# Streamed attention in slots of a whole product half, with values, transposes and scores of two stages after it

## The chip, the cores and the metric

The kernel runs on one core of a Trainium2 chip. The metric is the device time of one execution in microseconds (us); a kernel's time is the median of several runs. TensorE (PE) does matmuls and transposes, VectorE (DVE) and ScalarE (ACT) element work, GpSimd (POOL) some of the splitting of weights, and SyncE (SP) issues most of the DMAs.

## The reference

One layer of a model with two branches, on 1024 tokens of width 1024, all in float32:

```python
h = rmsnorm(x, norm_g) * (1 + scale) + shift
glu_a, glu_b, z_conv, q, k, v, z_att, g_conv, g_att = split(h @ w_in)
u = causal_conv31(glu_a * sigmoid(glu_b)) + conv_b
y_conv = (silu(layernorm(u)) * silu(z_conv)) @ w_conv_out
q, k = partial_rope(q), partial_rope(k)          # 24 heads of 64, 16 of 64 columns turned
for (window, dilation) in ((128, 1), (512, 4), (2048, 16)):   # 8 heads each
    out, max, den = causal window attention on every dilation-th token
att = sum(den * exp(max - max_all) * out) / sum(den * exp(max - max_all))
y_att = (att * silu(z_att)) @ w_att_out
merged = sigmoid(g_conv) * y_conv + sigmoid(g_att) * y_att
out = rmsnorm(x + gate * (merged @ w_o), final_g)
```

## The kernel before

Every float32 matrix that is multiplied is split into a high and a low part, and a tile's product is made of three matmuls (hi·hi, lo·hi, hi·lo; mm3, L72 to L75). A half of a unit, 128 output rows by 512 tokens, is 8 such products of three, thus 24 matmuls, summed in one PSUM bank. "Product" below means one of these matmuls of 128x512.

The stages follow each other: the norm and v, the units of the convolution branch, its output projection, then the attention stage (from about 645 to 1138 us), the merge and the last projection. The change is in the attention stage. There PE has two kinds of work at once:

- **A stream of units** (`units`, `pieces`). First 12 pairs of key and query units, one for each n = (j, g), j = 0 to 3 being a pair of heads and g = 0 to 2 the group; part 0 holds the columns that rope turns, part 1 the others. Then 8 units of the gate. Each unit has two halves. A half's bank comes from the pool pd2, which has two banks; so a half's first product waits until the half before the last has been read. After a half, `Parts.__call__` reads the bank: for part 0 a shuffle (L709), two multiplications (L710 "rot", L711) and an addition (L712) on DVE; then for both parts the high part on ACT (L720) and the low one on DVE (L721) into the tile kqp. Here "sh" and "rot" come from two buffers of one tag. So the rot of a unit's second half must wait until L720 and L721 of its first half have read theirs. When both halves are made, SP moves them by DMA (L785) to the tiles that attention reads: k2 and q2, and q's low part to ql.
- **Attention** (`Attend`), for the units that are finished, in eight stages per n; each takes two tiles of 128 queries of one head. `scores` (L843, L844) makes a bank of scores; DVE adds the mask and takes the maximum (L847) and its negative multiple nm (L850); ACT takes exp (L852, one instruction per tile, 128 or 256 wide). `turn` transposes the result (L860), and DVE or ACT copies it to pt (L863, L865). `values` multiplies with v (L875). After g = 2, `combine` loads the three groups' results again and weighs them, in two halves: small DVE work on maxima and denominators (L897 to L913), three wide multiplications (L917) and two additions (L920, L922, result "pr"), then four transposes on PE (L926), a multiplication by the silu gate (L927) and a store to DRAM (L929).

Both are put together in a loop over slots. A slot before has 12 products (k = 0 to 3, or 4 to 7 of a half), then the scores of stage st, the transposes of stage st−2, the values of stage st−3, then steps of `combine` by the tables FIRST and SECOND, and at last the call that reads a bank if a half is complete. A unit is 13 slots ahead of its attention (LEAD). The order of PE is written out by hand (`manual_schedule`); the order of DVE, ACT, POOL and SP is set by the scheduler when the kernel is built, and each engine then runs its list strictly in that order, waiting on semaphores.

## Time and profile before

| what | us |
|---|---|
| median of 3 runs (1286.51 to 1288.05) | 1287.0 |
| the profiled execution | 1284.9 |
| its span | 1283.1 |
| PE busy | 1251.0 |
| DVE busy | 895.0 |
| ACT busy | 476.3 |
| PE busy in the stretch 700 to 1060 us (360.0 long) | 355.88 |

The times are of one execution that a profiler recorded. A row of a timeline gives the start, the duration, the engine, the line, and output<-inputs; what stands in brackets is the engine's idle time before the instruction and what ended it. Matmuls are pipelined: a product lasts 0.39 us in the record, and the next one starts 0.23 us after it. "PE s L844 <- DMA ql<-kqp" in the list of waits means that PE's matmul of line 844, which writes s, waited for that DMA.

### The profile page before, as it was taken

The numbers are of one execution on the slowest core, as the hardware profiler recorded it, in microseconds if no ns is written. First come the engines' busy times: TensorE is split into PE (matmuls) and PEld (weight loads), VectorE is DVE, ScalarE is ACT, GpSimd is POOL, SyncE is SP. The second block draws the span as 40 slices with busy tenths as digits, with TensorE's granted clock in tenths as the row PEclk, the third lists the DMA queues.
The fourth block names the chain that finished last, engine by engine and source line by source line (L and its number), as shares of the span: only waits on it lengthen the run. The fifth ranks groups of instructions, "written<-read, shape, count | busy, mean of one in ns | idle before, by whom it ended". The sixth has DMA issues, their size and how long they took to land.

```text
span 1283.1 us, 16610 instructions
## 1 busy us (share of the span) xinstructions
PE 1251.0 (97%) x6148; PEld 1050.6 (82%) x6148; DVE 895.0 (70%) x1568; ACT 476.3 (37%) x911; POOL 114.6 (9%) x86
## 2 busy tenths in 40 slices
PE   6999999999999999999999999999999989999997
PEld 4777888888888888888788888888888878887786
DVE  6777999999999986853245545766666654348544
ACT  4653112111222146620115545445545458333211
POOL 0000000000000000000132111111111002202200
PEclk9999999999999999999999999999999999999999
DMA  9522311211211122555675565576675565558322
GB/s 367 180 97 73 109 66 57 91 52 47 94 55 50 50 74 74 165 183 188 143 182 125 125 159 142 156 179 150 153 207 126 147 181 177 151 203 286 117 96 69
DMA packets 85525, 171.53 MB, mean 134 GB/s; under 512 B 11202, under 2 KB 41026, under 8 KB 85444
## 3 DMA queue, kind: packets, MB, share of 16 engines
q1 hardware_dynamic: 69024, 157.66, 42.1%
q10 hardware_dynamic: 16420, 12.80, 3.2%
q8 instruction: 49, 0.80, 0.3%
q14 instruction: 32, 0.26, 0.1%
HBM read 105.74 MB, written 33.23 MB: 108 GB/s over the span
## 4 chain that ended last, share of the span: by engine, by line
PE 86%; DVE 5%; DMA 3%; issue 2%; ACT 2%; SPq 1%; POOL 1%; POOLq 0%; ACTq 0%; DVEq 0%
PE d L73 20%; PE d L74 20%; PE d L75 20%; PE o L875 4%; PE d L466 2%; PE d L467 2%; PE d L465 2%; PE d L1060 2%; PE d L1061 2%; PE t L860 2%; PE d L1059 2%; PE s L844 1%; PE s L843 1%; PE d L249 1%; PE d L247 1%
## 5 line engine op out<-in xcount | busy, mean ns | idle before, releaser
L73 PE MATMUL d<-hh,whi 128*128 128x512 f32 x1072 | 428.0, 399 | 1.8 <-DVE rot L710 0.9
L74 PE MATMUL d<-hl,whi 128*128 128x512 f32 x1072 | 418.0, 390 | 1.8 <-DVE hl L347 1.8
L75 PE MATMUL d<-hh,wlo 128*128 128x512 f32 x1072 | 419.1, 391 | 0.0
L406 DVE SCALAR_TENSOR_TENSOR v<-u,cw,v 128x1024 f32<-128x1024 f32 x232 | 280.7, 1287 | 0.0
L75 PEld LDWEIGHTS d<-hh,wlo 128*128 128x128 f32 x1072 | 201.3, 188 | 43.7 <-POOL wlo L58 0.7
L74 PEld LDWEIGHTS d<-hl,whi 128*128 128x128 f32 x1072 | 201.9, 188 | 41.6 <-DVE hl L347 2.6
L73 PEld LDWEIGHTS d<-hh,whi 128*128 128x128 f32 x1072 | 201.8, 188 | 41.3 <-DVE rot L710 1.5
L57 ACT ACTIVATE whi<-wraw 128x512 fp32r<-128x512 f32 (+1 forms) x107 | 87.9, 834 | 272.6 <-PE d L74 236.0
L58 POOL TENSOR_TENSOR wlo<-wraw,whi 128x512 fp32r<-128x512 f32 (+1 forms) x56 | 84.5, 1525 | 659.1 <-ACT whi L57 557.2
L852 ACT ACTIVATE sb<-sb,nm 128x128 f32<-128x128 f32 (+1 forms) x192 | 85.0, 444 | 86.3 <-DVE nm L850 82.0
L847 DVE CUSTOM_DVE_ANT_0 sb<-s,mask 128x128 f32<-128x128 f32 (+1 forms) x192 | 59.8, 347 | 61.1 <-PE s L844 54.9
L875 PE MATMUL o<-vt,pt 128*128 128x64 f32 x560 | 73.5, 267 | 1.6 <-ACT pt L863 1.0
L875 PEld LDWEIGHTS o<-vt,pt 128*128 128x128 f32 x560 | 70.2, 192 | 2.6 <-ACT pt L863 1.3
L58 DVE TENSOR_TENSOR wlo<-wraw,whi 128x1024 fp32r<-128x1024 f32 (+1 forms) x51 | 60.2, 1183 | 15.1 <-ACT whi L57 14.6
L1060 PE MATMUL d<-ol,hh 128*128 128x512 f32 (+1 forms) x136 | 51.6, 380 | 3.0 <-POOL ol L58 3.0
L844 PE MATMUL s<-k,ql 128*128 128x128 f32 (+1 forms) x192 | 51.0, 279 | 2.9 <-DMA ql<-kqp 2.9
L1059 PE MATMUL d<-oh,hh 128*128 128x512 f32 (+1 forms) x136 | 51.4, 378 | 0.1
L1061 PE MATMUL d<-oh,hl 128*128 128x512 f32 (+1 forms) x136 | 51.4, 378 | 0.0
L467 PE MATMUL d<-vh,hl 128*128 128x512 f32 x128 | 49.8, 389 | 0.0
L73 PE MATMUL d<-uh,whi 128*128 128x512 f32 x128 | 49.8, 389 | 0.0
L466 PE MATMUL d<-vl,hh 128*128 128x512 f32 x128 | 49.8, 389 | 0.0
L74 PE MATMUL d<-ul,whi 128*128 128x512 f32 x128 | 49.8, 389 | 0.0
(213 smaller groups left out, 1738.6 us busy)
## 6 DMA issues: line engine op xcount, KB each, us to landing
wraw<-in_w_t SPq DMA_DIRECT2D x67, 512.0 KB, 4.1
k<-kqp SPq DMA_DIRECT2D x96, 128.0 KB, 2.6
q<-kqp SPq DMA_DIRECT2D x96, 128.0 KB, 2.4
wa<-in_w_ada SPq DMA_DIRECT2D x16, 512.0 KB, 5.9
rd<-oscr SPq DMA_DIRECT2D x8, 792.0 KB, 5.6
ql<-kqp SPq DMA_DIRECT2D x48, 128.0 KB, 2.4
wraw<-in_w_v SPq DMA_DIRECT2D x11, 512.0 KB, 3.6
x<-in_xT SPq DMA_DIRECT2D x8, 512.0 KB, 10.2
```

The lines of the kernel that those rows point to most:

```text
L57: nc.scalar.activation(hi, raw, AF.Copy)
L58: (lo_eng or nc.vector).tensor_sub(lo, raw, hi.bitcast(F32))
L73: nc.tensor.matmul(ps, lh, rh, start=start, stop=False)
L74: nc.tensor.matmul(ps, lh, rl, start=False, stop=False)
L75: nc.tensor.matmul(ps, ll, rh, start=False, stop=stop)
L406: nc.vector.scalar_tensor_tensor(d, u[:, k:k + S], cw[:, ct, k:k + 1], d, op0=mult, op1=add)
L466: nc.tensor.matmul(ps, hh[:, k, ts_], rl, start=False, stop=False)
L852: nc.scalar.activation(sb[:, c:c + w], sb[:, c:c + w], AF.Exp, bias=nm[:, t - tp:t - tp + 1], scale=SCALE, accum_out=ov[:, t, h, 64:65])
L875: nc.tensor.matmul(self.po[:, t % 4, h], pt[:, c + i:c + i + P], self.vt[:, kb, r], start=i == 0, stop=i + P == w)
L1059: nc.tensor.matmul(ps, hh[:, k, c], rh, start=k == 0, stop=False)
L1060: nc.tensor.matmul(ps, hh[:, k, c], rl, start=False, stop=False)
L1061: nc.tensor.matmul(ps, hl[:, k, c], rh, start=False, stop=k == KT - 1)
```

## The change

- A slot is a whole half, 24 products. After it come the values of two stages, then the transposes of two stages, then the scores of two stages; the transposes are one slot behind the scores and the values two.
- LEAD is 7 slots of 24, and the tables FIRST and SECOND are given in new slots; the steps of one combination that were in slots of their own now often share one.
- The moves of q's low part come as soon as part 1 of its unit is made; v is loaded apart, in the third slot of the attention before (`load_v`).
- In `combine` the store to atscr is a step of its own, a slot later; for j = 3 that step isn't run.

```diff
@@ -768,8 +768,6 @@
                 for k in range(KT):
                     c = slice(k * P, (k + 1) * P)
                     mm3(ps, hi[:, c], lo[:, c], hh[:, k, s], hl[:, k, s], k == 0, k == KT - 1)
-                    if k == 3:
-                        yield
                 yield lambda half=half, s=s, ps=ps: consume(half, s, ps)
 
     LOW, UP = slice(0, 64), slice(64, 128)
@@ -798,6 +796,8 @@
 
         for part in range(2):
             move(q_low[n % 2], 0, n, part, 1, 1)
+
+    def load_v(n):
         v2[n] = stk.tile([P, 8, P], F32, name="vt", tag="vt", bufs=2)
         v_load(v2[n], order[n][1], order[n][0])
         if order[n][1] == 0:
@@ -925,10 +925,10 @@
         for t in range(4):
             nc.tensor.transpose(pt[:, t * P:(t + 1) * P], pr[:, t].rearrange("p h c -> p (h c)"), ident)
         nc.vector.tensor_mul(at, pt, at)
-        if j < 3:
-            nc.sync.dma_start(atscr[j][:, s], at)
-        else:
+        if j == 3:
             att_parts(3, s, at)
+        yield
+        nc.sync.dma_start(atscr[j][:, s], at)
         yield
 
     ah, al = {}, {}
@@ -942,54 +942,53 @@
     stream = pieces()
 
 
-    LEAD, TURN, VAL = 13, 2, 3
-    stages = 8 * len(order)
-
-    FIRST, SECOND = (2, 6, 6, 7, 7, 9), (8, 11, 11, 12, 12, 14)
+    LEAD = 7
+    slots = 4 * len(order)
+
+    FIRST, SECOND = (1, 3, 3, 3, 4, 4, 5), (5, 6, 6, 6, 7, 7, 8)
     beside, heads = {}, {}
 
     with tc.manual_schedule(engines={nc.tensor.engine}):
-        for slot_ in range(-LEAD, (2 * len(order) + KT) * 4 - LEAD):
+        for slot_ in range(-LEAD, (2 * len(order) + KT) * 2 - LEAD):
             due, made[:] = made[:], []
             after = next(stream)
             for x in due:
                 move_kq(*x)
-                if x == (0, 1):
-                    load_low(0)
-            if 0 <= slot_ < stages:
-                n, st_ = divmod(slot_, 8)
-                if st_ == 0:
-                    heads[n] = Attend(n)
-                if st_ == 4 and n + 1 < len(order):
-                    load_low(n + 1)
-                heads[n].scores(st_)
-            if TURN <= slot_ < stages + TURN:
-                n, st_ = divmod(slot_ - TURN, 8)
-                heads[n].turn(st_)
-            if VAL <= slot_ < stages + VAL:
-                n, st_ = divmod(slot_ - VAL, 8)
-                heads[n].values(st_)
-                if st_ == 7:
-                    del heads[n]
-                    j, g = order[n]
-                    if g == 2:
-                        for half, steps in enumerate((FIRST, SECOND)):
-                            c = combine(j, half)
-                            for x in steps:
-                                beside.setdefault(slot_ + x, []).append(c)
+                if x[1]:
+                    load_low(x[0])
+                    if x[0] == 0:
+                        load_v(0)
+            n, pair = divmod(slot_, 4)
+            if 0 <= slot_ < slots and pair == 0:
+                heads[n] = Attend(n)
+            if 0 <= slot_ < slots and pair == 2 and n + 1 < len(order):
+                load_v(n + 1)
+            for back, what in ((2, Attend.values), (1, Attend.turn), (0, Attend.scores)):
+                if 0 <= slot_ - back < slots:
+                    n, pair = divmod(slot_ - back, 4)
+                    for st_ in (2 * pair, 2 * pair + 1):
+                        what(heads[n], st_)
+                    if back == 2 and pair == 3:
+                        del heads[n]
+                        j, g = order[n]
+                        if g == 2:
+                            for half, steps in enumerate((FIRST, SECOND)):
+                                c = combine(j, half)
+                                for x in steps[:6 if j == 3 else 7]:
+                                    beside.setdefault(slot_ + x, []).append(c)
             for c in beside.pop(slot_, ()):
                 next(c)
             for c in late:
-                for x in (2, 2, 3):
+                for x in (1, 1, 2):
                     beside.setdefault(slot_ + x, []).append(c)
             late[:] = []
-            j = slot_ - stages - VAL
+            j = slot_ - slots - 2
             if 0 <= j < 3:
                 raw = load_raw(atscr[j])
                 for half in range(2):
                     s = slice(half * 512, half * 512 + 512)
                     att_parts(j, s, raw[:, s])
-            if j == 11:
+            if j == 5:
                 ahead = weights(a["w_ao"][0], 512)
             if after:
                 after()
```

The slots X that the prediction speaks of are numbered so that the attention starts with slot 0; slot 4m+2 holds the second half of a part 0. The next rows are of slot 19, X+1 for X = 18, and the first product of slot 20. The numbers behind the names tell tiles apart and are other ones in the two kernels.

PE before, at the end of the half ahead of the product that takes up the bank: s are scores, t transposes (t_6346 of exps, t_6355 of a combination), o the values, d the bank of products:

```order
L843 MATMUL s_6334<-k2_5884,q2_5885 128x128
L844 MATMUL s_6334<-k2_5884,ql_4284 128x128
L860 MATMUL t_6346<-ident_66,sb_6234 128x128 x3
L875 MATMUL o_6317<-vt_5747,pt_6315 128x64 x3
L926 MATMUL t_6355<-ident_66,pr_6259 128x128 x4
L73 MATMUL d_6364<-hh_64,whi_6058 128x512
```

PE after, at the same place:

```order
L860 MATMUL t_6267<-ident_66,sb_6184 128x128 x3
L860 MATMUL t_6273<-ident_66,sb_6196 128x128 x3
L843 MATMUL s_6279<-k2_5531,q2_5532 128x128
L844 MATMUL s_6279<-k2_5531,ql_4283 128x128
L843 MATMUL s_6279<-k2_5531,q2_5532 128x256
L844 MATMUL s_6279<-k2_5531,ql_4283 128x256
L843 MATMUL s_6291<-k2_5531,q2_5532 128x128
L844 MATMUL s_6291<-k2_5531,ql_4283 128x128
L843 MATMUL s_6291<-k2_5531,q2_5532 128x256
L844 MATMUL s_6291<-k2_5531,ql_4283 128x256
L73 MATMUL d_6327<-hh_64,whi_6024 128x512
```

Scores were first and are now last, directly ahead of the product d_6327, whose bank is that of d_6136, the second half of the unit's part 0.

DVE before at this place; rot_6160 is of the unit's first half, rot_6262 of the second, and d_6167 the bank that d_6364 above takes up:

```order
L847 ISA sb_6300,ov_5930<-s_6299,mask_4268 128x256
L847 ISA ov_5930 128x1
L850 TENSOR_SCALAR nm_6301<-ov_5930 128x2
L721 TENSOR_TENSOR kqp_5870<-rot_6160,kqp_5870 128x512
L710 TENSOR_TENSOR rot_6262<-d_6167,ctab_3672 128x512
L712 TENSOR_TENSOR rot_6262<-rot_6262,sh_6261 128x512
L847 ISA sb_6335,ov_6333<-s_6334,mask2_4269 128x128
```

DVE after; the same two are rot_6129 and rot_6211, and d_6136 is the bank that d_6327 takes up:

```order
L850 TENSOR_SCALAR nm_6281<-ov_5952 128x2
L847 ISA sb_6292,ov_5952<-s_6291,mask_4268 128x256
L847 ISA ov_5952 128x1
L850 TENSOR_SCALAR nm_6293<-ov_5952 128x2
L721 TENSOR_TENSOR kqp_5842<-rot_6129,kqp_5842 128x512
L710 TENSOR_TENSOR rot_6211<-d_6136,ctab_3672 128x512
L712 TENSOR_TENSOR rot_6211<-rot_6211,sh_6210 128x512
L721 TENSOR_TENSOR kqp_5842<-rot_6211,kqp_5842 128x512
L721 TENSOR_TENSOR kqp_6034<-d_6225,kqp_6034 128x512
```

The reading of the bank (L710) stands behind L721 of the first half in both; ahead of it are now the reductions of the scores s_6279 and s_6291, which PE issues just ahead of the product that needs the bank.

ACT before at this place, with the high part of the first half (L720 of rot_6160):

```order
L852 ACTIVATE sb_6300,ov_5930<-sb_6300,nm_6301 128x128
L852 ACTIVATE sb_6300,ov_5930<-sb_6300,nm_6301 128x256
L720 ACTIVATE kqp_5870<-rot_6160 128x512
L720 ACTIVATE kqp_5870<-rot_6262 128x512
L720 ACTIVATE kqp_6068<-d_6276 128x512
```

ACT after:

```order
L852 ACTIVATE sb_6280,ov_5952<-sb_6280,nm_6281 128x128
L852 ACTIVATE sb_6280,ov_5952<-sb_6280,nm_6281 128x256
L852 ACTIVATE sb_6292,ov_5952<-sb_6292,nm_6293 128x128
L852 ACTIVATE sb_6292,ov_5952<-sb_6292,nm_6293 128x256
L720 ACTIVATE kqp_5842<-rot_6129 128x512
L720 ACTIVATE kqp_5842<-rot_6211 128x512
L720 ACTIVATE kqp_6034<-d_6225 128x512
```

The first half's L720, on which L721 above waits, has four exps of the slot's own scores ahead of it in place of two.

The third place is the second half of the first combination (j = 0). DVE before, where pr_6259 is the operand of the transposes t_6355 above:

```order
L865 COPY pt_6249<-t_6245 128x384
L850 TENSOR_SCALAR nm_6235<-ov_5930 128x2
L922 TENSOR_TENSOR pr_6259<-rd_6054 128x512
L711 TENSOR_TENSOR sh_6261<-sh_6261,stab_3673 128x512
L847 ISA sb_6300,ov_5930<-s_6299,mask_4268 128x128
```

DVE after, where pr_6398 is that operand, in slot 20:

```order
L917 TENSOR_TENSOR rd_6208<-rd_6208,w_6306 128x4x2x64
L850 TENSOR_SCALAR nm_6386<-ov_6352 128x2
L920 TENSOR_TENSOR rd_6208<-rd_6208 128x4x2x64
L922 TENSOR_TENSOR pr_6398<-rd_6208 128x512
L927 TENSOR_TENSOR at_6312<-t_6400,at_6312 128x512
L709 STREAM_SHUFFLE sh_6502<-d_6419 128x512
```

PE after, at the end of slot 20:

```order
L843 MATMUL s_6384<-k2_5868,q2_5869 128x128
L844 MATMUL s_6384<-k2_5868,ql_4284 128x128
L926 MATMUL t_6400<-ident_66,pr_6398 128x128 x4
L73 MATMUL d_6419<-hh_64,whi_6218 128x512
L74 MATMUL d_6419<-hl_65,whi_6218 128x512
```

The scores s_6384, their reductions on DVE, pr and the transposes of pr are in one slot now; before, the transposes were in a later slot than pr, and behind transposes and values.

## Prediction

> **What bounds the kernel now.** I read the page first: the busy table, then the chain that ended last.

> ```profile
> span 1283.1 us, 16610 instructions
> PE 1251.0 (97%) x6148; PEld 1050.6 (82%) x6148; DVE 895.0 (70%) x1568; ACT 476.3 (37%) x911; POOL 114.6 (9%) x86
> PE 86%; DVE 5%; DMA 3%; issue 2%; ACT 2%; SPq 1%; POOL 1%; POOLq 0%; ACTq 0%; DVEq 0%
> ```

> TensorE is busy for 97% of the span and carries 86% of the last chain. The change leaves each matmul in the program, so it can win only PE's idle time or the joints between matmuls, and lose by making PE wait. Next I read PE's waits in the stretch of attention (672 to 1066 us):

> ```profile
> PE s L844 <- DMA ql<-kqp: 2.9, 1, 2.9
> PE o L875 <- ACT pt L863: 1.0, 1, 1.0
> PE d L73 <- DVE rot L710: 0.9, 4, 0.3
> PE o L875 <- DVE pt L865: 0.5, 1, 0.5
> ```

> In 394 us PE waits 5.3 us. That is all that a better order can win there. The third row matters most: four products waited, 0.3 us at most, for the rope's first multiplication (L710), which reads the PSUM bank that the product wants. There are two such banks.

> Then the timeline of PE through one slot of before (start, duration, line):

> ```profile
> 700.24 0.39 PE L75 MATMUL d<-hh,wlo 128*128 128x512 f32 x1
> ...
> 700.82 0.28 PE L844 MATMUL s<-k,ql 128*128 128x256 f32 x1
> 700.94 0.60 PE L860 MATMUL t<-ident,sb 128*128 128x128 f32 x4
> 701.37 1.00 PE L875 MATMUL o<-vt,pt 128*128 128x64 f32 x8
> 702.19 0.48 PE L73 MATMUL d<-hh,whi 128*128 128x512 f32 x1
> 702.50 0.39 PE L74 MATMUL d<-hl,whi 128*128 128x512 f32 x1
> 702.73 0.39 PE L75 MATMUL d<-hh,wlo 128*128 128x512 f32 x1
> ```

> From the last score (700.82) to the next product (702.19) lie 1.37 us of transposes and values. This is the time that DVE and ACT get after a stage's scores before PE needs a product's bank; after the products of a half's first slot they get another slot of 12 products.

> **The change part by part.** *Joints.* The first product after values passes on after 0.31 us (702.19 to 702.50), the second after 0.23 (to 702.73). A slot of 24 has one such joint where two of 12 had two: 48 joints less at 0.08 us are −4 us (bounds −8, if the score side saves as much, and 0).

> *Waits of before.* q's low part is moved with its unit, so the row of 2.9 us should go, and two stages of distance cover the two pt rows, 1.5 us. The rot waits (0.9) are counted anew below. I take −5, bounds −6 and −2.

> *The bank of a rope's second half.* This is the main term. A half's products go to the bank that the half two slots earlier used. Where that was the second half of a part 0 (X = 2, 6, ... 38: ten places), the bank comes free with L710, which writes "rot" into a buffer that L721 of the first half must have read; L721 waits for L720 on ACT. The order of the engines, given above, has these behind slot X+1's reductions, and in part behind its exps. In before 12 products, transposes and values stood between; this is the chain at one such place:

> ```profile
> 772.23 0.28 PE L844 MATMUL s<-k,ql 128*128 128x128 f32 x1
> ...
> 773.20 0.17 DVE L850 TENSOR_SCALAR nm<-ov 128x2 f32<-128x2 f32 x1
> ...
> 773.40 0.40 ACT L852 ACTIVATE sb<-sb,nm 128x128 f32<-128x128 f32 x1 [0.23 <-DVE nm L850]
> ...
> 773.80 0.39 ACT L852 ACTIVATE sb<-sb,nm 128x128 f32<-128x128 f32 x1
> ...
> 774.19 1.11 ACT L720 ACTIVATE kqp<-rot 128x512 fp32r<-128x512 f32 x1
> ...
> 775.33 1.09 DVE L721 TENSOR_TENSOR kqp<-rot,kqp 128x512 fp32r<-128x512 f32 x1 [1.96 <-ACT kqp L720]
> ```

> ```profile
> 776.45 0.69 DVE L710 TENSOR_TENSOR rot<-d,ctab 128x512 f32<-128x512 f32 x1
> 777.20 0.50 PE L73 MATMUL d<-hh,whi 128*128 128x512 f32 x1 [0.19 <-DVE rot L710]
> ```

> From the last score to the product it needed 772.23 to 777.20, 4.97 us, of which PE waited 0.19, since it had 4.8 us of other work. In after this work has gone to the other side: values and transposes come first, then two stages of scores, then at once the product. So the chain is a wait nearly as long as itself: about 4.97 less 0.2 that a product follows a score by anyway, 4.8.

> It varies with the unit and the order. Units of group 0 (X = 6, 18, 30) are contiguous and cheaper, and 256-wide tiles dearer:

> ```profile
> 844.86 0.63 ACT L720 ACTIVATE kqp<-rot 128x512 fp32r<-128x512 f32 x1 [1.13 <-DMA ql<-kqp]
> 845.52 0.69 DVE L721 TENSOR_TENSOR kqp<-rot,kqp 128x512 fp32r<-128x512 f32 x1 [2.81 <-ACT kqp L720]
> 846.25 0.69 DVE L710 TENSOR_TENSOR rot<-d,ctab 128x512 f32<-128x512 f32 x1
> 846.81 0.61 PE L926 MATMUL t<-ident,pr 128*128 128x128 f32 x4
> ```

> ```profile
> L847 DVE CUSTOM_DVE_ANT_0 sb<-s,mask 128x256 f32<-128x256 f32 x88 | 35.2, 420 | 21.1 <-PE s L844 21.1
> L847 DVE CUSTOM_DVE_ANT_0 sb<-s,mask 128x128 f32<-128x128 f32 x94 | 24.8, 285 | 31.7 <-PE s L844 25.5 <-PE t L860 6.1
> ```

> Contiguous saves 1.11−0.63 and 1.09−0.69, 0.9 us. The two stages of a slot queue on DVE: their eight short instructions add some 0.3 us of backlog at 285 ns tiles, and three 256-wide ones another 0.14 each. By the position of the first half's L720 on ACT:
> - behind all four exps (X = 10, 18, 26, 30): 5.0, 4.6, 5.8, 4.6, which is 4.8 plus backlog 0.2 to 1.0, less 0.9 and plus 0.7 for the contiguous ones with wide tiles: 20.0;
> - behind the first exp only (X = 2, 38): an exp less, 4.3 each: 8.6;
> - ahead of the exps (X = 14, 22): only the reductions (1.0), L721 (1.1) and L710 (0.7) with a little backlog are left, 3.1 each: 6.2;
> - a slot earlier, so that only L710 stands behind the reductions (X = 6, 34): 1.2 and 1.8: 3.0.

> Sum +38. Bounds: 33 if there is no backlog of the two stages, 44 if each place has a full backlog of a stage's reductions (0.6 us).

> *The combination's second half.* In after the four transposes L926 stand right behind the slot's scores (slots 20, 32, 44), and DVE computes their operand pr (L922) behind the same scores' reductions. In before:

> ```profile
> 833.61 0.28 DVE L847 CUSTOM_DVE_ANT_0 sb<-s,mask 128x128 f32<-128x128 f32 x1
> ...
> 834.89 0.32 DVE L913 TENSOR_TENSOR w<-w,wd 128x8 f32<-128x8 f32 x3
> 835.12 1.89 DVE L917 TENSOR_TENSOR rd<-rd,w 128x512 f32<-128x512 f32 x3
> 837.05 0.69 DVE L920 TENSOR_TENSOR rd<-rd 128x512 f32<-128x512 f32 x1
> ...
> 838.84 0.55 DVE L865 COPY pt<-t 128x384 f32<-128x384 f32 x1
> ...
> 840.19 0.68 DVE L922 TENSOR_TENSOR pr<-rd 128x512 f32<-128x512 f32 x1
> ```

> pr was ready at 840.87, its transposes ran at 846.81: 6 us of cover, so it cost nothing. In after DVE has from the end of the slot's transposes to do: the copy 0.55, then a stage's reductions with w, wd and L917 (833.61 to 837.01, 3.4), the second stage's reductions 0.75, L920 0.69, L922 0.68: 6.1 us. Scores of two stages are eight matmuls 0.12 us apart (700.82 to 700.94), 1.0 us, and a hop is 0.2: PE waits 6.1−1.0−0.2 = 4.9, in slots 20 and 32. In slot 44 the whole chain from ma on stands behind both stages' reductions: 1.3 us after the last score, then 3.9 for w, wd and L917, then 1.37: 6.5. Sum +16; bounds 11 (each a third shorter, if the scores start late enough for DVE to have done the first part) and 23 (the ACT exp in the middle and the two copies on top). The first halves (slots 17, 29, 41) have pr ahead of the turn copy: nothing.

> *Clock.* What PE does after such waits is in these rows, of the start and of the one long wait:

> ```profile
> 14.03 0.63 PE L247 MATMUL d<-wh,hh 128*128 128x512 f32 x1
> 14.46 0.63 PE L248 MATMUL d<-wl,hh 128*128 128x512 f32 x1
> ...
> 17.45 0.40 PE L249 MATMUL d<-wh,hl 128*128 128x512 f32 x1
> 17.68 0.39 PE L247 MATMUL d<-wh,hh 128*128 128x512 f32 x1
> ```

> ```profile
> 1052.68 0.30 PE L844 MATMUL s<-k,ql 128*128 128x128 f32 x1 [2.94 <-DMA ql<-kqp]
> 1052.81 0.28 PE L843 MATMUL s<-k,q 128*128 128x128 f32 x1
> ```

> After the idle start products are 0.43 us apart until 17.45 and 0.23 from there. After 2.94 us of waiting the next matmul follows at the usual 0.12 or so. No wait of 4 to 7 us inside the run exists in before. If such a wait brings the pace of 0.43 back for some 6 us, it costs 6×(1−0.23/0.43) = 2.8 us each; of the nine waits above 4 us I take three, +8. Bounds 0 and 20 (seven). [...]

> *At nothing.* The moves of q's low part are the same 48 DMAs from SP, half a unit earlier; atscr's store leaves a slot later and is read only after all attention; a lead of 7 slots of 24 against 13 of 12 is one half-slot. Of turn and values: from scores to their transposes there now lie 24 products plus the values, 24×0.23 = 5.5 us and more, against two slots in before; the exps end about 2 us after the last score (773.80+0.4 against 772.23), so they are covered.

> **Sum.** 1284.9, the profiled execution (its span and 1.8 us around it), −4 −5 +38 +16 +8 = 1337.9. The median of the runs stands 2.1 us above that execution: **1340 us**, 4% slower.

> **The rivals.**
> - A: the bank waits are hidden after all, if rot's buffers come free in time. Then −4 −5 +16 +5 on 1287.0: about 1299. Against it: the written order has L710 behind L721 behind the reductions of scores that PE has just issued.
> - B: the combination is hidden and the banks are not: −4 −5 +38 +5: about 1321. For it: in before it had 6 us of cover; against: its operand and its transposes are in one slot now.
> - C, the other side: both are hidden and only the savings are left, 1287.0−4−5 = 1278, faster. The mechanism is DVE's and ACT's own slack: DVE is busy 70%. It decides if the chain from last score to L710 fits into the time to the next product, 0.2 us now; the chain would have to fall from 4.97 to under 0.7 on average at 13 places, so I give it little.
> - D: the waits feed on: the exps' later end delays the transposes of the next slot (their ACT queue holds weights' splits too), or each long wait pulls the pace down. Ten further waits of 0.8 us, and seven drops at 2.8 in place of three: +8 +11 on 1340, about 1359.

> [...]

> **How the numbers follow.** Chances: the forecast 0.73, A 0.06, B 0.07, C 0.04, D 0.09. About 0.2% (2.6 us) is what a measurement of this kernel can tell from no change; only C is faster; a mixture in which small waits eat the savings, 0.01, would be the same: faster 0.04, same 0.01, slower 0.95. The forecast's own bounds: low 1340−5−5−8−4−1 = 1317 with all five terms at their low ends, high 1340+6+7+12 = 1365 with the three large ones at their high ends. B's 1321 and D's 1359 lie within, A and C are left out. Range 1318 to 1364.

> **What would show it.** Right: PE's waits have a row L73 <- DVE rot L710 of about 38 us over ten times, and a row for L926 <- DVE pr L922 of about 16 over three; the row of ql is gone. The pace after the waits (0.23 or 0.43 apart) settles the clock. Wrong: if the rot row is under 15 us, the bank term falls; if PE's idle grows by 50 us with other releasers, D's kind of wait was the cause; if it doesn't grow and the time still does, it is the clock.

## The result and the profile after

The changed kernel takes 1362.2 us (median of 5 runs, 1361.4 to 1363.7) against 1286.5 us of the kernel before in the same set of runs: a ratio of 1.059, interval 1.058 to 1.061. It is slower by 76 us. The prediction was 1340, its range 1318 to 1364: the direction and the main term were right, and two terms were far too small. The time lies 2 us under the end of the range and 22 us from the forecast.

From the page of the changed kernel's profiled execution (1363.65 us, span 1361.9):

```profile
span 1361.9 us, 16655 instructions
PE 1273.1 (93%) x6148; PEld 1067.8 (78%) x6148; DVE 886.0 (65%) x1568; ACT 476.5 (35%) x913; POOL 115.6 (8%) x86
PEclk9999999999999999999999989989989897999999
PE 87%; DVE 5%; ACT 2%; DMA 2%; issue 2%; SPq 1%; POOL 1%; POOLq 0%; ACTq 0%; DVEq 0%
```

The same 6148 matmuls are busy for 22 us more than before (1273.1 against 1251.0), and the row of the granted clock has tenths below 9 only in the attention stage. So there are two losses: PE waits more, and it is slower at the same work. The list of PE's waits in that stage, 645 to 1220 us:

```profile
PE d L73 <- DVE rot L710: 38.9, 11, 5.8
PE t L926 <- DVE pr L922: 23.2, 3, 11.8
```

The row of 2.9 us on ql is gone; the bank row has grown from 0.9 to 38.9, and a row of the combination has come, which before had none. Here is the first place, X = 2, in the timelines of PE, ACT and DVE:

```profile
708.05 0.28 PE L844 MATMUL s<-k,ql 128*128 128x256 f32 x1
712.72 0.79 PE L73 MATMUL d<-hh,whi 128*128 128x512 f32 x1 [4.39 <-DVE rot L710]
713.31 0.63 PE L74 MATMUL d<-hl,whi 128*128 128x512 f32 x1
713.74 0.63 PE L75 MATMUL d<-hh,wlo 128*128 128x512 f32 x1
...
718.43 0.63 PE L74 MATMUL d<-hl,whi 128*128 128x512 f32 x1
718.86 0.43 PE L75 MATMUL d<-hh,wlo 128*128 128x512 f32 x1
719.13 0.40 PE L73 MATMUL d<-hh,whi 128*128 128x512 f32 x1
719.36 0.40 PE L74 MATMUL d<-hl,whi 128*128 128x512 f32 x1
```

```profile
709.24 0.51 ACT L852 ACTIVATE sb<-sb,nm 128x256 f32<-128x256 f32 x1 [1.17 <-DVE nm L850]
...
709.75 1.05 ACT L720 ACTIVATE kqp<-rot 128x512 fp32r<-128x512 f32 x1
```

```profile
709.58 0.17 DVE L850 TENSOR_SCALAR nm<-ov 128x2 f32<-128x2 f32 x1
710.83 1.11 DVE L721 TENSOR_TENSOR kqp<-rot,kqp 128x512 fp32r<-128x512 f32 x1 [1.08 <-ACT kqp L720]
711.97 0.69 DVE L710 TENSOR_TENSOR rot<-d,ctab 128x512 f32<-128x512 f32 x1
```

The chain is the one that was forecast: last score, reductions, one exp, L720, L721, L710, product. Behind it 14 products follow at 0.43 us in place of 0.23, from 712.72 to 718.86. The same place in windows (start:end, length, busy PE, PEld, DVE, ACT, POOL, then the granted clock, the share of the DMA engines and GB/s):

```profile
707.00:713.00 6.00, 1.61 (x13) 1.41 (x12) 4.48 (x14) 4.49 (x12) 0.00 (x0) 0.92 0.00 0
713.00:719.00 6.00, 6.00 (x15) 4.64 (x16) 2.56 (x3) 1.18 (x2) 0.00 (x0) 0.51 0.53 117
719.00:725.00 6.00, 6.00 (x45) 5.51 (x44) 2.13 (x5) 2.62 (x4) 2.57 (x2) 1.00 0.42 85
```

PE is busy for the whole of both later windows, at a granted clock of 0.51 and of 1.00. The counts of matmuls, 15 and 45, are not of the same mix: the last window has 11 products and 34 short matmuls of attention. What compares is the spacing of products above, 0.43 against 0.23. A busy row alone does not show this; the granted clock beside it does.

The combination's second half in slot 44, in the timelines of DVE and of POOL:

```profile
1127.92 0.34 DVE L908 TENSOR_TENSOR wd<-w,rd 128x8 f32<-128x8 f32 x3 [1.15 <-ACT w L903]
...
1128.85 2.50 DVE L913 TENSOR_TENSOR w<-w,wd 128x8 f32<-128x8 f32 x3
1131.28 4.04 DVE L917 TENSOR_TENSOR rd<-rd,w 128x512 f32<-128x512 f32 x3
```

```profile
1128.91 4.65 POOL L58 TENSOR_TENSOR wlo<-wraw,whi 128x1024 fp32r<-128x1024 f32 x2 [24.34 <-ACT whi L57]
```

Three tiny L913 take 2.50 us in place of 0.32, and three L917 4.04 in place of 1.89, exactly while POOL splits two weights of 2.3 us each. In slot 20 one split does the same to L908 (DVE's row, then POOL's):

```profile
878.20 1.51 DVE L908 TENSOR_TENSOR wd<-w,rd 128x8 f32<-128x8 f32 x3
```

```profile
877.15 2.53 POOL L58 TENSOR_TENSOR wlo<-wraw,whi 128x512 fp32r<-128x512 f32 x2 [19.95 <-ACT whi L57]
```

In slot 44 L913 loses 2.2 us beside these splits; e8 below takes them from POOL.

**Where the time went.** For each kernel below I add its rows of PE's waits between 640 and 1250 us, and count the products (L73 to L75) that follow their predecessor by over 0.33 us without idle time between ("slow": the sum of what they take beyond 0.23). The column of slow products is good to some 0.5 us.

| kernel | span | PE's waits | slow products | span less both |
|---|---|---|---|---|
| before | 1283.1 | 9.6 | 0.5 | 1273.0 |
| changed | 1361.9 | 62.9 | 23.3 | 1275.7 |
| e1 later transposes | 1344.0 | 50.4 | 20.2 | 1273.4 |
| e2 sh elsewhere | 1336.6 | 44.2 | 19.0 | 1273.4 |
| e3 e1 and e2 | 1325.6 | 38.9 | 16.3 | 1270.4 |
| e4 scores first | 1326.8 | 39.7 | 15.4 | 1271.7 |
| e5 three buffers | 1366.3 | 69.4 | 18.4 | 1278.5 |
| e6 e1 and e5 | 1380.9 | 72.6 | 27.4 | 1280.9 |
| e8 gate's split on DVE | 1359.0 | 60.0 | 22.4 | 1276.6 |
| e9 three banks | 1356.7 | 63.4 | 16.7 | 1276.6 |
| e10 e1 and e9 | 1357.8 | 59.8 | 21.5 | 1276.5 |
| e12 block in mid-half | 1326.4 | 39.8 | 14.3 | 1272.3 |

The last column stays within 1270 to 1281 while the spans run from 1283 to 1381. So PE's waits and the slow pace behind them are the loss, in every one of these kernels, to about 5 us.

### The profile page after: what moved, and what is told of

It reads as the page before. It is cut to its first block, busy times and chain, and to the rows that moved or that the text cites. A ratio compares the mean times of both kernels' runs of the same rounds, so it can differ in the third digit from the quotient of the medians.

```text
span 1361.9 us, 16655 instructions
## 1 busy us (share of the span) xinstructions
PE 1273.1 (93%) x6148; PEld 1067.8 (78%) x6148; DVE 886.0 (65%) x1568; ACT 476.5 (35%) x913; POOL 115.6 (8%) x86
## 4 chain that ended last, share of the span: by engine, by line
PE 87%; DVE 5%; ACT 2%; DMA 2%; issue 2%; SPq 1%; POOL 1%; POOLq 0%; ACTq 0%; DVEq 0%
PE d L73 21%; PE d L74 21%; PE d L75 21%; PE o L875 4%; PE d L466 2%; PE d L467 2%; PE d L465 2%; PE t L860 2%; PE d L1059 2%; PE d L1060 2%; PE d L1058 2%; PE s L844 1%; PE s L843 1%; PE d L249 1%; DMA wraw<-in_w_o 1%
## 5 line engine op out<-in xcount | busy, mean ns | idle before, releaser
L73 PE MATMUL d<-hh,whi 128*128 128x512 f32 x1072 | 431.2, 402 | 39.8 <-DVE rot L710 38.9
L74 PE MATMUL d<-hl,whi 128*128 128x512 f32 x1072 | 426.4, 398 | 1.7 <-DVE hl L347 1.7
L75 PE MATMUL d<-hh,wlo 128*128 128x512 f32 x1072 | 425.3, 397 | 0.0
L406 DVE SCALAR_TENSOR_TENSOR v<-u,cw,v 128x1024 f32<-128x1024 f32 x232 | 280.4, 1278 | 0.0
L73 PEld LDWEIGHTS d<-hh,whi 128*128 128x128 f32 x1072 | 207.1, 193 | 85.2 <-DVE rot L710 41.2
L74 PEld LDWEIGHTS d<-hl,whi 128*128 128x128 f32 x1072 | 207.4, 193 | 44.4 <-DVE hl L347 2.5
L75 PEld LDWEIGHTS d<-hh,wlo 128*128 128x128 f32 x1072 | 206.4, 193 | 44.8
L57 ACT ACTIVATE whi<-wraw 128x512 fp32r<-128x512 f32 (+1 forms) x107 | 87.8, 833 | 303.9 <-PE d L74 264.5
L852 ACT ACTIVATE sb<-sb,nm 128x128 f32<-128x128 f32 (+1 forms) x192 | 84.3, 440 | 43.0 <-DVE nm L850 42.5
L865 DVE COPY pt<-t 128x384 f32<-128x384 f32 (+2 forms) x48 | 26.1, 544 | 103.6 <-PE t L860 103.5
L875 PEld LDWEIGHTS o<-vt,pt 128*128 128x128 f32 x560 | 70.0, 192 | 4.0
L875 PE MATMUL o<-vt,pt 128*128 128x64 f32 x560 | 67.8, 270 | 0.0
L847 DVE CUSTOM_DVE_ANT_0 sb<-s,mask 128x128 f32<-128x128 f32 (+1 forms) x192 | 59.7, 346 | 7.7 <-PE s L844 6.7
L465 PE MATMUL d<-vh,hh 128*128 128x512 f32 x128 | 49.8, 389 | 0.0
```

The source lines that it names most:

```text
L57: nc.scalar.activation(hi, raw, AF.Copy)
L73: nc.tensor.matmul(ps, lh, rh, start=start, stop=False)
L74: nc.tensor.matmul(ps, lh, rl, start=False, stop=False)
L75: nc.tensor.matmul(ps, ll, rh, start=False, stop=stop)
L406: nc.vector.scalar_tensor_tensor(d, u[:, k:k + S], cw[:, ct, k:k + 1], d, op0=mult, op1=add)
L465: nc.tensor.matmul(ps, hh[:, k, ts_], rh, start=k == 0, stop=False)
```

## The experiments

In kernels e2, e3, e4, e7 and e12 the edit shifts line numbers by some lines: L712 in e2 to e4 is the L710 of before, L928 the L926.

**e1: the transposes a slot behind pr.** Only the table moves, for j = 0 to 2:

```diff
-    FIRST, SECOND = (1, 3, 3, 3, 4, 4, 5), (5, 6, 6, 6, 7, 7, 8)
+    FIRST, SECOND = (1, 3, 3, 3, 4, 4, 5), (5, 6, 6, 6, 7, 8, 9)
```

> Changed kernel with the second half's transposes of a combination one slot behind pr, for j = 0 to 2 (SECOND 5,6,6,6,7,8,9). Theory (PE's waits, and the slow pace after each, are the whole loss): the three waits of 23.2 us and the 5.7 us that the slow products after them cost go: 1362 - 29 = 1333. Rival (the order of DVE only moves the wait to the next product or copy): over 1350, with a new row of waits of 15 us or more.

1345.7 us (ratio 1.047, interval 1.046 to 1.049), 16 us faster than the changed kernel. PE's waits:

```profile
PE d L73 <- DVE rot L710: 42.1, 11, 6.0
PE d L73 <- ACT whi L57: 3.8, 1, 3.8
...
PE d L75 <- POOL wlo L58: 1.7, 2, 1.2
```

The row of the combination is gone whole, so its cause is shown: pr and its transposes in one slot. A bit more than half of the gain arrived. The gate's weights are now waited for themselves (5.5 us, 5.0 of them where the changed kernel's PE stood for 11.8 us, in slot 44), and the bank row grew by 3.2.

**e2: sh elsewhere.** The shuffled copy goes into unwritten parts of kqp tiles, so that rot has both buffers:

```diff
-                sh, src = (ap_.tile([P, 512], F32, name=x, tag="gs", bufs=2) for x in ("sh", "rot"))
+                sh = (made_parts[self.n, 1].hi if half else self.lo)[:, s].bitcast(F32)
+                src = ap_.tile([P, 512], F32, name="rot", tag="gs", bufs=2)
```

> Changed kernel, the shuffled copy sh kept in parts of the kqp tiles that are not written yet, so that the two buffers hold only rot and the second half's L710 needn't wait for the first half's L721. Theory: the 38.9 us of the bank row and some 17 us of slow products after it go: 1362 - 56 = 1306, the combination's 23 us stay. Rival (the bank waits because scores stand last and DVE has their reductions to do first, whatever the buffers): the row of L73 <- DVE rot stays over 25 us and the time over 1340.

1340.8 us (1.044, 1.042 to 1.046). Neither theory: the bank row fell only from 38.9 to 32.7, and it is even now. Most of the 21 us came from elsewhere: PE's waits ahead of the combination's transposes fell from 23.2 to 7.3 us (6.4 on pr and 0.9 on pt).

```profile
PE d L73 <- DVE rot L712: 32.7, 11, 3.2
PE t L928 <- DVE pr L924: 6.4, 1, 6.4
```

Each of the eleven waits lies between 2.75 and 3.15 us. The second half's bank is in time now, but the scheduler put the first half's shuffle and multiplication behind the next scores' reductions, so that the first half's bank is late. In the same new list, slot 20 has pr (L924, at 876.01) ahead of the scores' reductions (from 878.65), and PE's wait there is 0.5 us in place of 5.7: in that place the order of DVE's list hides the combination.

**e3: both edits.**

> Both edits, e1 and e2, at once. Theory: 1362 - 29 - 56 = 1277, which is below the kernel before (1286.5) by the joints and by the waits of before that are gone. Rival (slots of 24 products cost time of their own, by longer queues on DVE and ACT): over 1295.

1327.0 us (1.032, 1.031 to 1.034), 35 us under the changed kernel, where e1 and e2 gained 16 and 21. That the totals nearly add up is partly chance, since each of the two edits takes most of the combination's wait. The combination's row is gone and the bank row of 32.6 us stays. The theory that the two causes removed would give 1277 was wrong by 50 us.

**e4: scores first.** Values and transposes stand behind the scores again. The edit of the order is shown; with it sh is staged as in e2, rot and the gate's tile have a single buffer, and exps have four:

```diff
-            for back, what in ((2, Attend.values), (1, Attend.turn), (0, Attend.scores)):
+            for back, what in ((0, Attend.scores), (2, Attend.values), (1, Attend.turn)):
```

> Changed kernel with the order scores, values, transposes in a slot, a fourth buffer for exps, and (to make room for it) sh in the kqp tiles and a single buffer for rot, so that the second half's L710 still waits for the first half's L721. Values (1.6 us) and transposes (0.9 us) then stand between the scores and the next product. Theory (a wait is the chain less what PE has to do beside it): each of the waits falls by 2.5 us, the bank row to some 15, the combination to some 16 us, the slow pace to about 10 us: some 1318. Rival (where the scores stand doesn't matter, the chain hangs on something else in the slot): 1362 within 10.

1328.7 us (1.034, 1.032 to 1.036), against 1318 expected and 1362 of the rival.

```profile
PE d L73 <- DVE rot L712: 24.5, 11, 3.6
PE t L928 <- DVE pr L924: 5.3, 1, 5.3
PE t L928 <- DVE pt L867: 4.4, 5, 1.7
```

The bank row falls to 24.5, the combination to 9.7 with what waits on pt. With sh staged as in e2 it is not the one edit alone. Against e2, which has the same staging but two buffers for rot and three for exps, the time falls by 12 us and the bank row by 8.2, 0.7 us at each place and not 2.5; the combination is 2.4 us above e2's 7.3. So where the scores stand matters, by less than the theory has it, as far as the changed buffers leave this open.

**e5: three buffers.** This was to be the clean form of e2 (the gate's tile of the same tag has three buffers as well):

```diff
-                sh, src = (ap_.tile([P, 512], F32, name=x, tag="gs", bufs=2) for x in ("sh", "rot"))
+                sh, src = (ap_.tile([P, 512], F32, name=x, tag="gs", bufs=3) for x in ("sh", "rot"))
-            sb = self.sb[st_] = ap_.tile([P, 512], F32, name="sb", tag="sb", bufs=3)
+            sb = self.sb[st_] = ap_.tile([P, 512], F32, name="sb", tag="sb", bufs=2)
```

> Changed kernel with three buffers in place of two for sh and rot (paid by two in place of three for exps). The second half's L710 then reuses the buffer of the first half's sh, which L712 has read long before, and the scheduler puts it ahead of the next scores' reductions. Theory (the buffer is what makes the bank late): the bank row of 38.9 us and the 17 us of slow products behind it go, the three waits of the combination stay: 1362 - 56 = 1306. Rival (slots of 24 with the scores last make some half's bank late anyway, as e2 did with the first half's): 25 us or more of L73 waits stay, over 1335.

1367.4 us (1.063, 1.062 to 1.065): 5 us slower than the changed kernel. The row of L710 is gone, and others have taken its place:

```profile
PE t L926 <- DVE pr L922: 33.3, 3, 11.8
PE d L73 <- DVE kqp L721: 26.8, 6, 6.3
```

ACT and DVE at the first of the new places:

```profile
682.64 1.15 ACT L57 ACTIVATE whi<-wraw 128x512 fp32r<-128x512 f32 x2 [9.74 <-PE d L74]
683.69 1.96 ACT L720 ACTIVATE kqp<-rot 128x512 fp32r<-128x512 f32 x2
```

```profile
684.80 2.87 DVE L721 TENSOR_TENSOR kqp<-rot,kqp 128x512 fp32r<-128x512 f32 x2 [8.80 <-ACT kqp L720]
```

With rot free for longer, the scheduler put both L720 of the unit behind a split of weights (L57) that itself waits 9.74 us for PE. The unit's L721 come late, and behind them the L721 that reads part 1's bank. My theory that the buffer alone is what makes the bank late falls here: it is one of several things that can. The exps lost a buffer in the same edit. No wait of DVE in this trace is that of a reduction (L847) for a transpose, but what the lost buffer did to the lists was not tried apart.

**e6: e1 and e5.**

> e5 and the transposes of e1 together. Theory: 1362 - 56 - 29 = 1277, up to 1285 if the gate's weights come late as they did in e1 (5.5 us of waits there): at or under the kernel before. Rival (the slots of 24 have a price beyond these two waits): over 1295.

1378.7 us (1.072, 1.071 to 1.074), the slowest of all.

```profile
PE d L73 <- DVE kqp L721: 49.8, 10, 6.3
```

**e7: q's low part alone,** in the kernel before:

```diff
-                if x == (0, 1):
-                    load_low(0)
+                if x[1]:
+                    load_low(x[0])
+                    if x[0] == 0:
+                        load_v(0)
```

> Kernel before with one part of the change alone: q's low part moved as soon as part 1 of its unit is made, v still loaded at stage 4. Theory: the one wait of 2.9 us on ql goes and nothing else moves: 1285.3 - 3 = 1282, ratio 0.998. Rival (the moves collide with the others on SP's queue and delay k2 and q2, or the order of ACT and DVE shifts): 1288 or more.

1285.6 us, ratio 0.9999 (0.9989 to 1.0008): nothing that can be measured, so the theory's 0.998 falls, and so does the rival's 1288. A wait on ql of 1.3 us is left, and two on the gate's weights have come, of 1.7 and 1.0 us.

**e8: the gate's split on DVE.**

```diff
-            yield weights(a["w_t"][60 + d], lo_eng=nc.gpsimd), gate(d)
+            yield weights(a["w_t"][60 + d]), gate(d)
```

> Changed kernel with the gate weights' low part made by DVE in place of POOL. In the changed kernel three L913 (128x8) took 2.50 us and three L917 4.04 us in slot 44, in place of 0.32 and 1.89, while POOL did two splits of 2.3 us each. Theory (DVE's two-input instructions stand still while POOL works): they take about 0.3 and 2.0 us again; two splits of 1.2 us now stand on DVE ahead of pr, so the wait of 11.8 us becomes 11.8 - 4.3 + 2.4 = 9.9. Rival (they are long for another reason, the DMAs or the clock): 2.5 and 4.0 us as before, wait about 14.

1360.8 us (1.058, 1.056 to 1.060). The total hardly moves, since DVE now has the two splits itself, but the durations in slot 44 are the theory's:

```profile
1128.81 0.32 DVE L913 TENSOR_TENSOR w<-w,wd 128x8 f32<-128x8 f32 x3
1129.05 1.29 DVE L917 TENSOR_TENSOR rd<-rd,w 128x512 f32<-128x512 f32 x2
1130.25 1.22 DVE L58 TENSOR_TENSOR wlo<-wraw,whi 128x1024 fp32r<-128x1024 f32 x1
1131.38 0.69 DVE L917 TENSOR_TENSOR rd<-rd,w 128x512 f32<-128x512 f32 x1
```

0.32 and 1.98 us, and the wait of that slot is 9.7 where 9.9 was expected. POOL's work is shown to be what stretched them. The theory's words, two inputs and standing still, are wider than the rows: in the changed kernel an L721, which has two inputs as well, took 0.69 us at 877.59, inside POOL's split of 877.15, and the L721 of this shape without POOL's work took 0.69 too.

**e9: three banks for products,** and one for the values' results:

```diff
-    pd = c_ctx.enter_context(psum_pool("pd2", bufs=2))
+    pd = c_ctx.enter_context(psum_pool("pd2", bufs=3))
-                self.po = psa.tile([P, 4, 2, 64], F32, name="o", tag="o")
+                self.po = psa.tile([P, 4, 2, 64], F32, name="o", tag="o", bufs=1)
```

> Changed kernel with three banks for products in place of two (one bank for the values' results in place of two). A product then needs the bank of the half three slots back, so every reader has a slot of 24 products (5.5 us) more. Theory as it stands after e5 (any reader of a bank that stands behind a slot's scores on DVE or ACT is late by 1 to 6 us, because the product follows the scores at once and there are only two banks): the bank row of 38.9 us and some 17 us of slow products go, the combination's waits stay at 23 and its pace: 1362 - 56 = 1306. Rival (the engines' lists put the readers later still, as they did in e5, or the values wait for their one bank): over 1335 with 25 us of waits on L710, L721 or L878.

1358.6 us (1.057, 1.055 to 1.059). The bank row falls to a third, and the combination takes what it gave:

```profile
PE t L926 <- DVE pr L922: 41.1, 5, 11.8
PE d L73 <- DVE rot L710: 13.3, 6, 3.9
PE d L73 <- ACT whi L57: 6.1, 1, 6.1
```

Two first halves of the combination wait now as well. The rival was right on the time, if not on the row.

**e10: e1 and e9.**

> e9 and the later transposes of e1 at once. Theory: 1306 less what e1 gained, 16 to 29: 1277 to 1290, at or under the kernel before. Rival (slots of 24 have a price of their own): over 1300.

1363.0 us (1.060, 1.058 to 1.062). No expected gain came: the waits are 21.5 us on L710, 13.8 on the gate's weights and 21.5 ahead of the combination's transposes.

**e11: three banks in the kernel before.**

> Kernel before with the same three banks: the control for e9. Theory (in slots of 12 the bank is late by 0.9 us in all): ratio 0.998 to 1.002. Rival (banks bound the kernel before too): under 0.995.

1287.5 us, ratio 1.0009 (1.0000 to 1.0018). In slots of 12 the banks bind nothing, as the theory has it.

**e12: the block in the middle of a half,** with e1's table:

```diff
                     mm3(ps, hi[:, c], lo[:, c], hh[:, k, s], hl[:, k, s], k == 0, k == KT - 1)
+                    if k == 3:
+                        yield
...
-            after = next(stream)
+            next(stream)
...
+            after = next(stream)
             if after:
```

> e1 (later transposes of the combination) with the whole block of values, transposes and scores moved from the end of a half to its middle, behind k = 3: after the scores come 12 products into the same bank, 2.75 us, before a product needs another. Theory (a wait is the chain from the last score to the bank's reader, less what PE has to do in that time): the bank row of e1, 42.1 us over eleven places, falls by 2.75 us at each to about 15; slow products fall to some 5 us since only waits over about 2 us brought them; the gate's late weights, 5.5 us, stay. With 1277 for PE's work: some 1304. Rival (a slot's readers are late because the engines' lists put them late, as in e5, e6 and e10, and cover doesn't help): bank row over 30 us, time over 1330.

1330.5 us (1.035, 1.034 to 1.036), 15 us under e1.

```profile
PE d L73 <- DVE rot L710: 24.0, 10, 3.1
PE d L73 <- ACT whi L57: 4.7, 1, 4.7
```

The bank row falls from 42.1 to 24.0, some 1.7 us at each place where 2.75 were expected: midway between theory and rival. The time is the rival's, over 1330, where the theory had 1304; two waits of 1.9 us ahead of the combination's transposes have come as well. Cover on PE helps, and the engines' lists, which the scheduler writes anew for each kernel, take a part of it back: at the first place (PE waits until 712.00) L720 stands behind all four exps, where in the changed kernel it stood behind the first.

None of these kernels beats the kernel before.

## Why the prediction was right, and where it was not

**The bank of a rope's second half: right, place by place.** PE's idle time in brackets at each place, against the working:

| X | 2 | 6 | 10 | 14 | 18 | 22 | 26 | 30 | 34 | 38 |
|---|---|---|---|---|---|---|---|---|---|---|
| forecast | 4.3 | 1.2 | 5.0 | 3.1 | 4.6 | 3.1 | 5.8 | 4.6 | 1.8 | 4.3 |
| measured | 4.4 | 1.2 | 4.9 | 3.5 | 4.5 | 2.5 | 5.8 | 4.6 | 2.3 | 4.4 |

Together 38.1, and 0.8 at one product ahead of the attention: 38.9 against 38. The mechanism is the forecast one: the chain could be read from the one place of before where PE had waited 0.19 us for it, since the engines' lists of the changed kernel said what would be ahead of what.

**The combination: right in place, too small.** 5.7, 5.7 and 11.8 us against 4.9, 4.9 and 6.5; 23.2 against 16. The step that failed is the cost of DVE's chain, worked out from durations in which POOL was idle. In slots 20 and 32 one split made L908 take 1.51 us in place of 0.34. In slot 44 POOL's two splits added 2.2 us to L913 and 2.15 to L917; and w's exp stood on ACT behind a slot's four exps (1.15 us of waiting at L908, against 0.29 before). These exps were themselves held up, since ACT, coming from the gate's sigmoid, first loaded a table, while nm was ready at 1125.47:

```profile
1124.84 1.28 ACT L852 ACT_TABLE_LOAD   x1
```

**The clock: the largest error.** +23 against +8. I had taken three drops among nine waits above 4 us, and that wait of 2.94 us in the kernel before, which cost nothing, for the rule. In the changed kernel all twelve waits above 2.2 us brought the slow pace, with 1.3 to 2.9 us lost each (2.8 were forecast). So the step that failed is the number of drops: twelve, at 1.9 us each on average. One of the two shortest, PE's timeline:

```profile
1039.86 0.79 PE L73 MATMUL d<-hh,whi 128*128 128x512 f32 x1 [2.26 <-DVE rot L710]
1040.45 0.63 PE L74 MATMUL d<-hl,whi 128*128 128x512 f32 x1
...
1043.01 0.48 PE L74 MATMUL d<-hl,whi 128*128 128x512 f32 x1
1043.33 0.40 PE L75 MATMUL d<-hh,wlo 128*128 128x512 f32 x1
```

So a wait of 2.26 us was enough here, where the forecast counted only waits above 4. The rival D's second half, that each long wait pulls the pace down, was what happened; its first half, ten further waits of 0.8 us, was not.

The records of the granted clock say what the length of a wait alone does not. In each of the fourteen kernels the clock changes only between 1.0 and 0.5, and only at times that lie a whole multiple of 3.413 us apart, to within 3 ns (27 changes in the changed kernel, one in the kernel before). So I cut the time of each run at these multiples into windows of 3.413 us, called the grid here, and PE's idle time in a window (its length less busy PE) can be held against the clock of the next. First the wait of 2.26 us above, then that of 2.94 us in the kernel before:

```profile
1036.37:1039.78 3.41, 1.23 (x12) 1.09 (x10) 2.24 (x6) 1.77 (x3) 0.00 (x0) 1.00 0.00 0
1039.78:1043.19 3.41, 3.33 (x8) 2.65 (x9) 2.58 (x11) 2.54 (x10) 0.00 (x0) 0.50 0.10 20
```

```profile
1048.26:1051.68 3.42, 1.48 (x8) 1.02 (x6) 0.00 (x0) 3.08 (x7) 0.00 (x0) 1.00 0.75 175
1051.68:1055.09 3.41, 2.41 (x19) 2.35 (x20) 1.14 (x6) 2.17 (x5) 0.00 (x0) 1.00 0.98 229
```

The shorter wait left 2.18 us of one window idle, and the clock was 0.50 in the next; the longer one was split by the grid into 1.94 and 1.00 us, and the clock stayed. Even 1.94 is at the edge: of the windows with 1.8 to 2.0 us of idle time in all fourteen kernels, 16 of 18 were followed by a drop. That the wait of before cost nothing was a matter of where it fell, and no rule for the forecast.

**The joints.** −4 forecast, and about −1 found. From one half's first product to the next's, the five undisturbed slots with 12 values and 6 transposes take 8.34 us twice (the first from 733.52) and 8.43 three times, and pairs of slots of before with the same work 8.39 to 8.44, but for one of 8.60. Slots with 8 values and 4 transposes take 7.63 to 7.68, pairs of before 7.67 or 7.68, but for one of 7.83. Apart from these two, that is 0.03 us a slot or less.

**The waits of before.** −5 forecast, and the rows are gone. But e7 shows that moving q's low part early is worth nothing by itself in the kernel before; other waits of the same size came.

The sum with the measured terms: 1284.9 −1 −5 +38.9 +23.2 +23.3 = 1364.3, against 1363.65 of the profiled execution.

**Where the range held by luck.** The combination (23.2) just and the clock (23.3) clearly lie above the upper bounds that the prediction gave them, 23 and 20. The time is within the range all the same because the bank term stayed 5 us under its own bound of 44.

**What stays open.** That the loss is PE's waits and the slow pace is shown by the table. The combination's wait has a shown cause, the order of its steps, since e1 removes it. That the bank's wait has one removable cause is not shown: in e5, with a third buffer, another reader was late in its place; in e9 and e10, with a third bank, L710 was still late at six and nine places (13.3 and 21.5 us), and other waits grew. What they have in common, that a product follows two stages of scores at once and that the lists of DVE and ACT put some reader of its bank behind these scores' work, is supported by e4 and e12, where cover on PE took 8 to 18 us off the row; but cover alone didn't remove it. A kernel in which the lists of DVE and ACT have the bank's readers first wasn't tried; e2's slot 20, where DVE's list has pr first, shows only for the combination what this can do.

## What to carry to other kernels

Merging small slots into large ones saves very little at the joints (0.03 us a slot or less here) and takes away the cover that small slots gave: ask for each wait that PE doesn't have now what it does between the producer's input and the consumer. A wait of 0.2 us in the profile before is a chain that just fits, and its whole length is what a reordering can expose. Where a scheduler writes the other engines' lists, removing one dependence changes them all, so read the new lists before expecting the wait to be gone; and count a wait of PE above some 2 us at its length and 1.3 to 2.9 us more, as the twelve of the changed kernel cost, knowing that between some 2 and 4 us it depends on how the wait falls whether the extra comes.
